# Entry of a hybrid encoder layer in another order: projections of the first half of the tokens ahead of the norm of the second, and a norm by square root and one Newton step

## The chip, the cores and the metric

The program runs on one core of one Trainium2 chip. The metric is the device time of one execution, in microseconds. The kernel before was timed three times: 1414.19, 1415.23 and 1418.97 us, median 1415.23 us.

## The reference

One layer of an encoder over 1024 tokens with 1024 channels, then a last norm. What matters here is the way in:

```
h = rms_norm(x, g_mix[l])
z = h @ w_in[l]
u_fn, q, k, v, u_ssm, gate_logits = jnp.split(z, splits, axis=-1)
y_fn = fourier_mix(u_fn) @ w_br_fn[l]
y_na = neighbourhood_attention(q * q_scale, k, v, na_rpb[l]) @ w_br_na[l]
y_ssm = ssm_branch(u_ssm, ssm_a_re[l], ...) @ w_br_ssm[l]
merged = gates[:, :, 0] * y_fn + gates[:, :, 1] * y_na + gates[:, :, 2] * y_ssm
x = x + merged @ w_out[l]
h = rms_norm(x, g_ffn[l])
x = x + jnp.square(jax.nn.relu(h @ w_up[l])) @ w_down[l]
```

rms_norm divides a token by the root of the mean of its squares. ssm_branch turns its parameters (log step, decay, B, C) into complex powers and phases, independent of x, and then scans the input u_ssm over the tokens.

## The kernel before

Each fp32 product is made of three matmuls in a rounded format: an operand is cut into a high part (a cast on ScalarE, ACT) and a low part (a subtraction on VectorE, DVE), `w_cut` for weights (L142, L143), `norm_b` for activations (L199, L200). Tokens lie in eight tiles of 128, in two halves of four.

The entry of `run` does this for each half: `norm_a` per tile (a Square with a row sum on ACT, L219; the inverse root on DVE, L208 to L212; a scaling in place on DVE, L221), `norm_b` per group of 128 channels (four transposes on TensorE, PE, L228, then the cut into hT), and the projection of the state space input u (two weights, 48 matmuls, `proj`), whose result ACT copies to uT (L940). Then come eight tiles of attention values v, 24 matmuls each, and then the gate logits and the rest.

The inverse root `rstd` is an integer estimate and three Newton steps on DVE, seven small instructions after the scale, eight in all.

The state space branch is a generator, `ssm`, that the main loop steps: 0.4 steps for every third matmul. Its first part, `ssm_params`, is some 110 operations on [128, 16] numbers, nearly all on GpSimd (POOL), each waiting for the one before; they begin when the parameters ssv have been loaded. Where DVE continues that chain, its first instruction is the complex square of L356 (recorded as L239), which uses the scratch columns T(4) and T(5) that POOL's last products (L239 to L244) use. The phases (`ssm_turn_a`, `ssm_turn_b`: tiles ef, en, E) go through DVE and ACT beside it.

All loads go through SyncE's queue (SP) in the order of issue. Weights are loaded into four buffers of their own (`wp`).

Every engine runs its own instructions in a fixed order. That order isn't the order of the source text: when the program is built, a planner with a timing model of its own orders each engine's instructions, and an engine that waits at one instruction holds up all behind it.

Of the kernel before, what the change touches and what calls it, by code (L numbers as in the profile page):

```python
# [23 lines left out]
NK = 128  # L24
# [40 lines left out]
class Trunk:  # L65
# [137 lines left out]
    def rstd(self, ss):  # L203


        V = self.nc.vector
        y, h, t = (self.tiny([P, 1], F32, x, 4) for x in ("ry", "rh", "rt"))
        V.tensor_scalar(out=h, in0=ss, scalar1=-0.5 / D, scalar2=-0.5 * EPS, op0=ALU.mult, op1=ALU.add)  # L208
        V.tensor_scalar(out=y.bitcast(I32), in0=h.bitcast(I32), scalar1=-0.5, scalar2=519526879.0, op0=ALU.mult, op1=ALU.add)
        for _ in range(3):  # L210
            V.scalar_tensor_tensor(out=t, in0=y, scalar=h, in1=y, op0=ALU.mult, op1=ALU.mult)
            V.scalar_tensor_tensor(out=y, in0=t, scalar=1.5, in1=y, op0=ALU.add, op1=ALU.mult)  # L212
        return y

    def norm_a(self, x, h=None):

        q = self.s([P, D], F32, "h") if h is None else h
        ss = self.tiny([P, 1], F32, "ss", 4)
        self.nc.scalar.activation(q, x, AF.Square, accum_out=ss)  # L219
        h = x if h is None else h  # L220
        self.nc.vector.tensor_scalar_mul(h, x, self.rstd(ss))  # L221
        return h
# [44 lines left out]
    def ssm_params(self):  # L267
# [46 lines left out]
        sn, sh, cs = T(6), T(7), T(8)  # L314
        nc.scalar.activation(sn, w, AF.Sin)
        nc.scalar.activation(sh, w, AF.Sin, scale=0.5)
        for q in range(4):
            self.ssm_turn_b(q)
        TT(T(4), sh, sh, ALU.mult)
        TS(cs, T(4), -2.0, 1.0, ALU.mult, ALU.add)  # L320
        lr, li = T(9), T(10)
# [98 lines left out]
    def ssm_prep(self, q):  # L420

        nc, V, G, A = self.nc, self.nc.vector, self.nc.gpsimd, self.nc.scalar
        g0 = 4 * q
        gs = slice(g0, g0 + 4)
        pa, bbar, bhat = self.ssm_pa, self.ssm_bb, self.ssm_bh

        def product(out, x, y, sh):

            t = self.m(sh, F32, "pt")
            V.tensor_tensor(out=t, in0=x[1], in1=y[1], op=ALU.mult)  # L430
            V.tensor_tensor(out=out[:, 0], in0=x[0], in1=y[0], op=ALU.mult)
            yield
            V.tensor_tensor(out=out[:, 0], in0=out[:, 0], in1=t, op=ALU.subtract)
            V.tensor_tensor(out=t, in0=x[1], in1=y[0], op=ALU.mult)
            yield
            V.tensor_tensor(out=out[:, 1], in0=x[0], in1=y[-1], op=ALU.mult)
            V.tensor_tensor(out=out[:, 1], in0=out[:, 1], in1=t, op=ALU.subtract if len(y) == 3 else ALU.add)
            yield

        U = self.m([P, 4, NK], F32, "U")  # L440
        self.dma(U, self.u_scr[64 * q:64 * q + 64].rearrange("(g c) (s k) -> (c s) g k", g=4, k=NK))
        AA = self.s([P, 2, 4, 8, 16], F32, "AA")
        sh = [P, 4, 8, 16]
        yield from product(AA, [self.ssm_cc[:, i, gs, :].unsqueeze(2).to_broadcast(sh) for i in range(2)],
                           [pa[:, i, gs, :].unsqueeze(3).to_broadcast(sh) for i in range(3)], sh)
        BB = self.s([P, 2, 4, 16, 8], F32, "BB")
        sh = [P, 4, 16, 8]
        yield from product(BB, [bhat[:, i, gs, :].unsqueeze(3).to_broadcast(sh) for i in range(2)],
                           [pa[:, i, gs, ::-1].unsqueeze(2).to_broadcast(sh) for i in range(2)], sh)
        AA = AA.rearrange("p i g s c -> p i g (s c)")  # L450
        bz = self.m([P, 2, 4, 64], F32, "bz")
        G.memset(bz, 0.0)
        for i in range(2):
            A.copy(bz[0:64, i, :, 0:16], bbar[0:64, i, gs, :])
            A.copy(bz[64:128, i, :, 32:48], bbar[64:128, i, gs, :])
        yield
        for _ in range(6 if q == 0 else 0):
            yield
        BT = self.s([P, 4, 2, P], F32, "BT")
        for b in range(2):  # L460
            ps = self.ps([P, 2, 2, P])
            for j in range(2):
                for i in range(2):
                    nc.tensor.transpose(ps[:, j, i, :], BB[:, i, 2 * b + j].rearrange("p c s -> p (c s)"), self.ident)  # L464
            A.copy(BT[:, 2 * b:2 * b + 2], ps)
# [12 lines left out]
        V.tensor_tensor(out=kp[:, :, 7, :], in0=kp[:, :, 7, :], in1=kt, op=ALU.add)  # L478
        yield
        M = self.m([P, 4, P], F32, "M")  # L480
        for s in range(8):
            self.dma(M[s::8], kp[:, :, 7 - s:15 - s, :].rearrange("p g t c -> p g (t c)"))
        yield
        self.ssm_mat[q] = (AA, BT, M, U)

    def ssm_data(self, q):
# [24 lines left out]
        V.tensor_tensor(out=ta, in0=ta, in1=tb, op=ALU.add)  # L511
        V.tensor_tensor(out=tc_, in0=tc_, in1=td, op=ALU.subtract)
        yield
        zs = [self.m(sh, F32, "z") for _ in range(2)]
        for v, z in ((ta, zs[0]), (tc_, zs[1])):
            V.tensor_tensor_scan(out=flat(z)[0:64, 1:L], data0=flat(rz)[0:64, 0:L - 1], data1=flat(v)[0:64, 0:L - 1],
                                 initial=0.0, op0=ALU.mult, op1=ALU.add)
# [3 lines left out]
                                 data1=flat(v)[64:128, 1:L][:, ::-1], initial=0.0, op0=ALU.mult, op1=ALU.add)  # L521
            V.memset(z[64:128, :, NK - 1], 0.0)
            yield
        V.tensor_tensor(out=ta, in0=zs[0], in1=E[:, 0], op=ALU.mult)
        V.tensor_tensor(out=tb, in0=zs[1], in1=E[:, 1], op=ALU.mult)
        yield
        V.tensor_tensor(out=td, in0=zs[1], in1=E[:, 0], op=ALU.mult)
        V.tensor_tensor(out=tc_, in0=zs[0], in1=E[:, 1], op=ALU.mult)
        yield
        V.tensor_tensor(out=ta, in0=ta, in1=tb, op=ALU.subtract)  # L530
        V.tensor_tensor(out=tc_, in0=tc_, in1=td, op=ALU.add)
# [35 lines left out]
    def ssm(self):  # L567
# [7 lines left out]
                yield from self.ssm_prep(q)  # L575

        def data():
            for q in range(4):
                while q not in self.ssm_mat:
                    yield  # L580
                yield from self.ssm_data(q)
# [314 lines left out]
    def run(self):  # L896
# [11 lines left out]
        def load_x():  # L908
            xs.append(self.s([P, D], F32, "x"))
            t = len(xs) - 1  # L910
            self.dma(xs[t], self.a["x"][t * P:(t + 1) * P, :])

        load_x()
        self.consts()
        for _ in range(3):
            load_x()
        self.w_raw(0)
        self.w_raw(1)
        for _ in range(4):
            load_x()  # L920
        hT = []
        uts = [self.s([P, 8, NK], F32, "uT") for _ in range(2)]
        for t in range(4):
            self.norm_a(xs[t])
        self.w_cut(0)
        for half in range(2):
            hT.append(self.act_tiles(half, "hT"))
            for k in range(8):
                self.norm_b(xs[4 * half:4 * half + 4], hT, half, k, self.gs[:, 0])
                if half == 0 and k == 3:  # L930
                    self.w_cut(1)
            xs[4 * half:4 * half + 4] = [None] * 4
            if half == 0:
                ws = self.w_next(2, 0, 1)
                for t in range(4, 8):
                    self.norm_a(xs[t])

            for i in range(2):
                ps = self.proj(ws[i], hT, half)
                A.copy(uts[i][:, :, 64 * half:64 * half + 64].rearrange("p s k -> p k s"), ps.rearrange("p (k s) -> p k s", s=8))  # L940
        ssm = Side(self.ssm(), 0.4)
        del xs
        for i in range(2):
            self.dma(self.u_scr[P * i:P * i + P], uts[i].rearrange("p s k -> p (s k)"))
        del uts, ws

        wv = self.w_next(4, 1, 2)
        self.sides.append(ssm)
        for t in range(8):
# [13 lines left out]
        del wv, rh, rl  # L963

        heads = {}

# [654 lines left out]
```

## Time and profile before

| | |
|---|---|
| median of the runs | 1415.23 us |
| profiled execution | 1414.49 us |
| its span in the trace | 1412.7 us |
| PE busy | 1378.5 us, 98% |
| DVE, ACT, POOL busy | 67%, 41%, 12% |

The span is the time from the first to the last instruction of the trace; 1.8 us of the profiled execution lie outside it. A time stamp below is in us from the start of the span. Instructions of one engine in the timeline may overlap by some hundredths, since they are pipelined.

### The profile page before, as it was taken

Reading aid. Unit: us, or ns where it says so; the run is one execution under the profiler, and the core shown is the slowest. Engines: PE = TensorE matmul, PEld = TensorE weight load, DVE = VectorE, ACT = ScalarE, POOL = GpSimd, SP = SyncE. Lnnn points to the kernel's source line nnn. Section 1 sums busy time; section 2 is a strip of 40 time slices with the busy share of each in tenths; the row PEclk is TensorE's granted clock in tenths of the full one; section 3 lists DMA queues with packets and bytes.
Section 4 is the critical chain, followed back from the end, with each engine's and each line's share of the span. In section 5 each row is a group of like instructions: output and inputs, shape, how many; then the busy total and the mean of one; then the engine's idle time right before and its main releaser. Section 6 shows DMA issues by size and latency. Waiting matters only on the chain.

```text
span 1412.7 us, 18521 instructions
## 1 busy us (share of the span) xinstructions
PE 1378.5 (98%) x6520; PEld 1150.1 (81%) x6520; DVE 952.8 (67%) x1812; ACT 577.0 (41%) x1103; POOL 166.8 (12%) x345
## 2 busy tenths in 40 slices
PE   6999999999999999999999999999999999999997
PEld 5788878888888888888788788888888788888885
DVE  6768788767562315443516897677777999878667
ACT  5523464766552212122403664233333454444244
POOL 3800122322200000000000012121121100000000
PEclk9999999999999999999999999999999999999999
DMA  6352546665652219111433125444448886363303
GB/s 230 107 161 83 171 120 196 187 176 154 210 194 98 100 45 331 57 56 49 136 111 142 68 90 202 148 164 144 154 149 282 282 278 199 118 191 127 97 9 119
DMA packets 103436, 209.65 MB, mean 148 GB/s; under 512 B 18224, under 2 KB 34992, under 8 KB 103344
## 3 DMA queue, kind: packets, MB, share of 16 engines
q1 hardware_dynamic: 79872, 153.10, 33.2%
q0 software_dynamic: 23472, 55.38, 12.0%
q8 instruction: 51, 0.84, 0.2%
q14 instruction: 41, 0.34, 0.1%
HBM read 146.52 MB, written 56.62 MB: 144 GB/s over the span
## 4 chain that ended last, share of the span: by engine, by line
PE 71%; issue 18%; POOL 5%; DVE 2%; DMA 2%; ACT 1%; SPq 0%; POOLq 0%; DVEq 0%
PE ps L171 42%; PE ps L165 25%; POOL h_scr L1300 4%; PE ps L792 1%; PE ps L809 1%; PE ps L813 1%; DMA ssv<-in_ssm_v 1%; DMA wr<-in_w_in 1%; SPq L111 0%; PE ps L1088 0%; DMA yT<-y_scr 0%; POOL pt L249 0%; DMA h_scr<-hs 0%; PE ps L464 0%; POOL pt L250 0%
## 5 line engine op out<-in xcount | busy, mean ns | idle before, releaser
L165 PE MATMUL ps<-dw,dh 128*128 128x512 f32 x1344 | 306.1, 390 | 2.3 <-DVE dw L197 2.3
L165 PE MATMUL ps<-fb,uw 128*128 128x512 f32 x1344 | 306.6, 390 | 1.4 <-DVE t L1147 1.0
L165 PEld LDWEIGHTS ps<-dw,dh 128*128 128x128 f32 x1344 | 252.1, 188 | 55.6 <-DVE dw L197 3.1
L165 PEld LDWEIGHTS ps<-fb,uw 128*128 128x128 f32 x1344 | 252.0, 188 | 54.5 <-PE ps L1088 1.2
L171 PE MATMUL ps<-hTh,wh 128*128 128x512 f32 x576 | 231.5, 403 | 3.2 <-DVE hTl L200 1.6
L171 PE MATMUL ps<-hTl,wh 128*128 128x512 f32 x576 | 227.1, 395 | 1.3 <-DVE hTl L200 1.3
L171 PE MATMUL ps<-hTh,wl 128*128 128x512 f32 x576 | 227.5, 395 | 0.0
L171 PEld LDWEIGHTS ps<-hTh,wh 128*128 128x128 f32 x576 | 109.3, 190 | 24.2 <-ACT wh L142 2.4
L171 PEld LDWEIGHTS ps<-hTh,wl 128*128 128x128 f32 x576 | 108.9, 189 | 23.0 <-issue 0.2
L171 PEld LDWEIGHTS ps<-hTl,wh 128*128 128x128 f32 x576 | 109.1, 189 | 20.9 <-DVE hTl L200 1.8
L143 DVE TENSOR_TENSOR wl<-wr,wh 128x1024 fp32r<-128x1024 f32 (+2 forms) x76 | 70.7, 942 | 60.2 <-ACT wh L142 57.4
L196 ACT CAST dh<-da 128x512 fp32r<-128x512 f32 x112 | 69.4, 620 | 96.9 <-PE ps L165 61.2
L1384 DVE TENSOR_TENSOR x<-x,ps 128x512 f32<-128x512 f32 x112 | 73.8, 687 | 33.8 <-PE ps L165 33.7
L197 DVE TENSOR_TENSOR dh<-da,dh 128x512 fp32r<-128x512 f32 x112 | 77.4, 691 | 14.9 <-ACT dh L196 14.8
L1300 POOL DMA_DIRECT2D h_scr<-hx x48 | 26.0, 541 | 495.6 <-ACT hx L1270 375.5
L171 PE MATMUL ps<-act,wh 128*128 128x512 f32 x256 | 78.7, 390 | 0.1
L142 ACT CAST wh<-wr 128x1024 fp32r<-128x1024 f32 (+2 forms) x76 | 60.7, 821 | 32.3 <-PE ps L171 8.3
L196 ACT CAST uw<-us 128x512 fp32r<-128x512 f32 x64 | 38.1, 626 | 84.2 <-DVE us L1227 84.2
L1022 ACT ACTIVATE tg<-ps 128x512 f32<-128x512 f32 x32 | 19.1, 597 | 123.9 <-PE ps L171 118.5
L1272 DVE SCALAR_TENSOR_TENSOR hx<-hx 128x512 f32<-128x512 f32 x52 | 35.8, 689 | 40.2 <-ACT hx L1264 39.7
L196 ACT CAST dw<-wd 128x512 fp32r<-128x512 f32 x80 | 49.4, 618 | 19.1 <-PE ps L165 18.4
L171 PEld LDWEIGHTS ps<-act,wh 128*128 128x128 f32 x256 | 47.7, 188 | 10.0 <-ACT wh L142 0.5
(288 smaller groups left out, 2092.5 us busy)
## 6 DMA issues: line engine op xcount, KB each, us to landing
da<-h_scr SPq DMA_DIRECT2D x112, 256.0 KB, 3.4
wr<-in_w_in SPq DMA_DIRECT2D x36, 512.0 KB, 4.4
wu<-in_w_up SPq DMA_DIRECT2D x32, 512.0 KB, 3.6
h_scr<-hs POOLq DMA_DIRECT2D x64, 256.0 KB, 2.6
wd<-in_w_down SPq DMA_DIRECT2D x64, 256.0 KB, 3.8
bm<-in_rpb POOLq DMA_DIRECT2D x64, 192.0 KB, 4.8
h_scr<-hx POOLq DMA_DIRECT2D x48, 256.0 KB, 2.7
vj<-v_scr POOLq DMA_DIRECT2D x32, 256.0 KB, 6.5
```

The lines of the kernel that those rows point to most:

```text
L142: self.nc.scalar.copy(hi, r)
L143: self.nc.vector.tensor_tensor(out=lo, in0=r, in1=hi.bitcast(F32), op=ALU.subtract)
L165: self.nc.tensor.matmul(out=out, lhsT=l, rhs=r, start=start and i == 0, stop=stop and i == last, skip_group_check=more)
L171: self.nc.tensor.matmul(out=out, lhsT=l, rhs=r, start=i == 0, stop=i == last)
L196: nc.scalar.copy(hi, src)
L197: nc.vector.tensor_tensor(out=lo, in0=src, in1=hi.bitcast(F32), op=ALU.subtract)
L792: nc.tensor.transpose(ps[:, i, :], sm[:, i * P:(i + 1) * P], self.ident)
L809: nc.tensor.matmul(out=ps, lhsT=v, rhs=two[i][x], start=i == 0 and x == 0, stop=False)
L1022: A.activation(tg, ps, AF.Tanh, scale=0.5)
L1272: V.scalar_tensor_tensor(out=x, in0=x, scalar=0.0, in1=x, op0=ALU.max, op1=ALU.mult)
L1300: self.nc.gpsimd.dma_start(out=self.t.h_scr[c, j - 1], in_=x)
L1384: self.nc.vector.tensor_tensor(out=self.x1[t][:, cs], in0=self.x1[t][:, cs], in1=self.banks[j][q], op=ALU.add)
```

## The change

The first four tiles of x are loaded, then two weights for u, then the parameters of the state space branch, then two weights for v; the other four tiles of x are loaded later. The order in the source is now: norm of the first half, u of the first half, v of the first tile, v of tiles 1 to 3 with the norm of the second half stepped in between as a side generator, u of the second half, v of tiles 4 to 7. The state space branch is stepped by hand in the entry, and its part that needs u waits for a flag. The inverse root is now a Sqrt on ACT, a reciprocal on DVE and one Newton step; a Sqrt of a constant stands at the start of the kernel, ahead of all data. Squares go to buffers that are there anyway. In the scan of the state space branch two buffers are saved.

```diff
--- before.py
+++ after.py
@@ -206,15 +206,15 @@
         V.tensor_scalar(out=h, in0=ss, scalar1=-0.5 / D, scalar2=-0.5 * EPS, op0=ALU.mult, op1=ALU.add)
-        V.tensor_scalar(out=y.bitcast(I32), in0=h.bitcast(I32), scalar1=-0.5, scalar2=519526879.0, op0=ALU.mult, op1=ALU.add)
-        for _ in range(3):
-            V.scalar_tensor_tensor(out=t, in0=y, scalar=h, in1=y, op0=ALU.mult, op1=ALU.mult)
-            V.scalar_tensor_tensor(out=y, in0=t, scalar=1.5, in1=y, op0=ALU.add, op1=ALU.mult)
+        self.nc.scalar.activation(y, h, AF.Sqrt, scale=-2.0)
+        V.reciprocal(y, y)
+        V.scalar_tensor_tensor(out=t, in0=y, scalar=h, in1=y, op0=ALU.mult, op1=ALU.mult)
+        V.scalar_tensor_tensor(out=y, in0=t, scalar=1.5, in1=y, op0=ALU.add, op1=ALU.mult)
         return y
...
@@ -454,8 +450,11 @@
-        for _ in range(6 if q == 0 else 0):
+        while not self.u_done:
             yield
+        U = self.m([P, 4, NK], F32, "U")
+        self.dma(U, self.u_scr[64 * q:64 * q + 64].rearrange("(g c) (s k) -> (c s) g k", g=4, k=NK))
...
@@ -910,43 +914,41 @@
+        one = self.tiny([P, 1], F32, "one", 1)
+        V.memset(one, 1.0)
+        A.activation(one, one, AF.Sqrt)
         load_x()
         self.consts()
         for _ in range(3):
             load_x()
         self.w_raw(0)
         self.w_raw(1)
-        for _ in range(4):
-            load_x()
-        hT = []
+        ssm = Side(self.ssm(), 0.4)
+        ssm.step()
+        self.w_raw(2)
+        self.w_raw(3)
+        self.u_done = False
+        hT = [self.act_tiles(0, "hT")]
         uts = [self.s([P, 8, NK], F32, "uT") for _ in range(2)]
         for t in range(4):
-            self.norm_a(xs[t])
+            self.norm_a(xs[t], q=uts[0].rearrange("p s k -> p (s k)"))
         self.w_cut(0)
...
+        def second():
+
+            for t in range(4, 8):
+                self.norm_a(xs[t], q=self.wp.tile([P, D], F32, tag="w", name=self.name("h")))
+                yield
+            for _ in range(4):
+                yield
+            for k in range(8):
+                self.norm_b(xs[4:8], hT, 1, k, self.gs[:, 0])
+                yield
+
+        u_in(0)
+        wv = self.w_next(4, 0, 0)
+        for t in range(4):
+            if t == 1:
+                for _ in range(4):
+                    load_x()
+                hT.append(self.act_tiles(1, "hT"))
+                norm2 = self.side(second(), 0.67)
+            if t > 0:
+                ssm.step()
+            v_in(t)
+        norm2.finish()
+        del xs
+        ssm.step()
+        ssm.step()
+        self.sides.append(ssm)
+        u_in(1)
+        for i in range(2):
+            self.dma(self.u_scr[P * i:P * i + P], uts[i].rearrange("p s k -> p (s k)"))
+        del uts, ws
+        self.u_done = True
+        for t in range(4, 8):
+            if t == 5:
+                self.w_ahead(1, 2)
+            v_in(t)
```

On DVE, this is where the scaling of the first tile of the second half and the state space chain stood before (x_89 is that tile; ry its inverse root; ef, en, E the phases; pt the parameters):

```order
L221 TENSOR_SCALAR x_89<-x_89,ry_236 128x1024
...
L221 TENSOR_SCALAR x_95<-x_95,ry_281 128x1024
L200 SCALAR_TENSOR_TENSOR hTl_346<-ps_353,gs_77,hTh_345 128x512
L402 TENSOR_TENSOR ef_588<-ssk_513,konst_75 128x512
...
L404 TENSOR_SCALAR en_607<-en_607 128x512
L239 TENSOR_TENSOR pt_511<-pt_511 128x16
```

And now (x_366 is the same tile, wl the low part of a weight for v, vt the values of the first tile, pa the powers at the chain's end):

```order
L400 TENSOR_TENSOR ef_428<-ssk_102,konst_78 128x512
L403 TENSOR_TENSOR ef_416<-ef_416,en_417 128x512
L143 TENSOR_TENSOR wl_322<-wr_143,wh_321 128x1024
...
L197 TENSOR_TENSOR vt_362<-ps_337,vt_362 128x8x64
L239 TENSOR_TENSOR pt_100<-pt_100 128x16
...
L366 TENSOR_SCALAR pa_704<-pa_704 128x128
L221 TENSOR_SCALAR x_366<-x_366,ry_444 128x1024
```

The scaling of the second half's tiles stood ahead of the first instruction of the phases and now stands behind the chain's DVE part, from L239 to L366; the first weight for v is cut behind the first phases.

On PE, the end of the first u before, and what follows it (ps_353 and its like are transposes of the second half):

```order
L171 MATMUL ps_319<-hTl_170,wh_199 128x512
L171 MATMUL ps_319<-hTh_169,wl_200 128x512
L228 MATMUL ps_353<-konst_75,x_89 128x128
L228 MATMUL ps_360<-konst_75,x_89 128x128
L228 MATMUL ps_367<-konst_75,x_89 128x128
```

And now the place where the second half's transposes begin, which is behind the first three tiles of v (ps_337, ps_434, ps_530; ps_603 is the fourth):

```order
L171 MATMUL ps_530<-wl_334,hTh_153 128x512
L171 MATMUL ps_530<-wh_333,hTl_154 128x512
L228 MATMUL ps_549<-konst_78,x_366 128x128
L228 MATMUL ps_559<-konst_78,x_366 128x128
L171 MATMUL ps_603<-wh_321,hTh_147 128x512
```

The 72 matmuls of three tiles of v now stand between the first u and the first transpose of the second half; the fourth tile's matmuls, the second u and the other four tiles stand behind it.

## Rows read from the trace of the kernel before

**Rows 1.** The page: busy us of each engine, share of the span, and number of instructions.

```profile
PE 1378.5 (98%) x6520; PEld 1150.1 (81%) x6520; DVE 952.8 (67%) x1812; ACT 577.0 (41%) x1103; POOL 166.8 (12%) x345
```

**Rows 2.** The waits of PE over the whole span: who, for whom, us in total, times, longest.

```profile
PE ps L228 <- DVE rh L208: 10.0, 1, 10.0
PE ps L171 <- DVE hTl L200: 2.9, 3, 1.3
PE ps L792 <- DVE mx L767: 1.1, 1, 1.1
PE ps L809 <- ACT sm L774: 0.8, 1, 0.8
PE ps L792 <- DVE sm L784: 0.6, 1, 0.6
```

**Rows 3.** Stretches of one us: their length, busy time of PE, PEld, DVE, ACT and POOL with counts, granted clock of PE (1.00 is 2.4 GHz, 0.50 is 1.2 GHz), DMA share, GB/s.

```profile
36.00:37.00 1.00, 0.00 (x0) 0.00 (x0) 1.00 (x3) 1.00 (x3) 0.83 (x3) 1.00 0.04 8
38.00:39.00 1.00, 1.00 (x4) 0.81 (x3) 1.00 (x4) 0.98 (x2) 0.83 (x3) 0.50 0.00 0
40.00:41.00 1.00, 1.00 (x4) 0.81 (x3) 1.00 (x4) 1.00 (x2) 0.75 (x4) 0.59 0.04 8
...
191.00:192.00 1.00, 0.61 (x3) 0.64 (x4) 0.97 (x3) 0.95 (x4) 0.87 (x2) 0.51 0.00 0
197.00:198.00 1.00, 1.00 (x4) 0.78 (x3) 1.00 (x1) 0.00 (x0) 0.00 (x0) 0.58 0.00 0
```

**Rows 4.** The timeline of PE: start, busy time, instruction, count, and in brackets the idle time before it and what ended it. The last row is the first matmul behind all values.

```profile
18.75 0.50 PE L171 MATMUL ps<-hTh,wh 128*128 128x512 f32 x1 [0.80 <-DVE hTl L200]
...
29.77 3.98 PE L228 MATMUL ps<-konst,x 128*128 128x128 f32 x32
34.55 0.50 PE L171 MATMUL ps<-hTh,wh 128*128 128x512 f32 x1 [0.80 <-DVE hTl L200]
...
87.25 1.96 PE L165 MATMUL ps<-AA,bz 128*64 128x128 f32 x16
...
95.41 0.39 PE L171 MATMUL ps<-hTh,wh 128*128 128x512 f32 x1
```

**Rows 5.** The timeline of DVE in the first norm: the second Newton step of the first tile, the next tile's first instruction, the low part of the first weight, and the scaling of the fourth tile.

```profile
6.37 0.22 DVE L211 SCALAR_TENSOR_TENSOR rt<-ry,rh 128x1 f32<-128x1 f32 x1
8.48 0.15 DVE L208 TENSOR_SCALAR rh<-ss 128x1 f32<-128x1 f32 x1 [1.89 <-ACT h L219]
...
12.59 1.22 DVE L143 TENSOR_TENSOR wl<-wr,wh 128x1024 fp32r<-128x1024 f32 x1
...
15.17 0.75 DVE L221 TENSOR_SCALAR x<-x,ry 128x1024 f32<-128x1024 f32 x1
```

**Rows 6.** SP's issues of loads (start and length of the issue), and the chain that ended last (start, length): the load of the first weight and that of the parameters, each from issue to landing.

```profile
4.62 3.00 SPq L111 DMA_DIRECT2D x<-in_x  x4
...
11.09 0.33 SPq L111 DMA_DIRECT2D ssv<-in_ssm_v  x1
...
3.54 7.53 DMA wr<-in_w_in
11.09 9.20 DMA ssv<-in_ssm_v
```

**Rows 7.** The timeline of POOL in the parameter chain: its first instruction, two that follow each other beside a DVE instruction that reads PSUM, one beside a DVE weight cut, and its last before the products on larger tiles.

```profile
20.38 0.20 POOL L256 TENSOR_SCALAR pt<-ssv 128x16 f32<-128x16 f32 x1 [18.43 <-DMA ssv<-in_ssm_v]
...
41.53 0.22 POOL L250 TENSOR_TENSOR pt<-pt 128x16 f32<-128x16 f32 x1
41.84 0.30 POOL L249 TENSOR_SCALAR pt<-pt 128x16 f32<-128x16 f32 x1
...
44.63 1.02 POOL L250 TENSOR_TENSOR pt<-pt 128x16 f32<-128x16 f32 x1
...
62.44 0.22 POOL L244 TENSOR_TENSOR pt<-pt 128x16 f32<-128x16 f32 x1
```

**Rows 8.** The timeline of DVE where it goes on with that chain, and a stretch in which it works beside POOL.

```profile
43.22 2.35 DVE L143 TENSOR_TENSOR wl<-wr,wh 128x1024 fp32r<-128x1024 f32 x2
...
62.69 0.58 DVE L239 TENSOR_TENSOR pt<-pt 128x16 f32<-128x16 f32 x1 [6.26 <-POOL pt L244]
63.28 1.11 DVE L405 TENSOR_TENSOR ef<-ef,en 128x512 f32<-128x512 f32 x1
...
68.28 0.68 DVE L197 TENSOR_TENSOR vt<-ps,vt 128x512 fp32r<-128x512 f32 x1
69.15 0.42 DVE L417 TENSOR_SCALAR E<-en 128x512 f32<-128x512 f32 x1
71.48 0.23 DVE L368 TENSOR_SCALAR pa<-pa 128x128 f32<-128x128 f32 x1
```

**Rows 9.** The timeline of ACT: copies of u, a cast of a weight for v, a load of a function table, and the wait of a Sin for POOL.

```profile
29.51 2.00 ACT L940 COPY uT<-ps 128x512 f32<-128x512 f32 x2 [2.46 <-PE ps L171]
...
37.60 1.09 ACT L142 CAST wh<-wr 128x1024 fp32r<-128x1024 f32 x1
38.70 1.28 ACT L316 ACT_TABLE_LOAD   x1
40.00 0.22 ACT L316 ACTIVATE pt<-pt 128x16 f32<-128x16 f32 x1
...
46.62 0.22 ACT L315 ACTIVATE pt<-pt 128x16 f32<-128x16 f32 x1 [3.58 <-POOL pt L249]
```

More of the change, by code (lines that the diff above doesn't have):

```diff
@@ L208, in rstd, with norm_a @@
         V.tensor_scalar(out=h, in0=ss, scalar1=-0.5 / D, scalar2=-0.5 * EPS, op0=ALU.mult, op1=ALU.add)
-        V.tensor_scalar(out=y.bitcast(I32), in0=h.bitcast(I32), scalar1=-0.5, scalar2=519526879.0, op0=ALU.mult, op1=ALU.add)
-        for _ in range(3):
-            V.scalar_tensor_tensor(out=t, in0=y, scalar=h, in1=y, op0=ALU.mult, op1=ALU.mult)
-            V.scalar_tensor_tensor(out=y, in0=t, scalar=1.5, in1=y, op0=ALU.add, op1=ALU.mult)
-        return y
-    def norm_a(self, x, h=None):
-        q = self.s([P, D], F32, "h") if h is None else h
+        self.nc.scalar.activation(y, h, AF.Sqrt, scale=-2.0)
+        V.reciprocal(y, y)
+        V.scalar_tensor_tensor(out=t, in0=y, scalar=h, in1=y, op0=ALU.mult, op1=ALU.mult)
+        V.scalar_tensor_tensor(out=y, in0=t, scalar=1.5, in1=y, op0=ALU.add, op1=ALU.mult)
+        return y
+    def norm_a(self, x, h=None, q=None):
+        q = h if q is None else q
         ss = self.tiny([P, 1], F32, "ss", 4)
@@ L316, in ssm_params @@
         nc.scalar.activation(sh, w, AF.Sin, scale=0.5)
-        for q in range(4):
-            self.ssm_turn_b(q)
         TT(T(4), sh, sh, ALU.mult)
@@ L438, in product @@
             yield
-        U = self.m([P, 4, NK], F32, "U")
-        self.dma(U, self.u_scr[64 * q:64 * q + 64].rearrange("(g c) (s k) -> (c s) g k", g=4, k=NK))
         AA = self.s([P, 2, 4, 8, 16], F32, "AA")
@@ L513, in ssm_data @@
         yield
-        zs = [self.m(sh, F32, "z") for _ in range(2)]
+        zs = [tb, td]
         for v, z in ((ta, zs[0]), (tc_, zs[1])):
@@ L523, in ssm_data @@
             yield
-        V.tensor_tensor(out=ta, in0=zs[0], in1=E[:, 0], op=ALU.mult)
-        V.tensor_tensor(out=tb, in0=zs[1], in1=E[:, 1], op=ALU.mult)
+        V.tensor_tensor(out=ta, in0=tb, in1=E[:, 0], op=ALU.mult)
+        V.tensor_tensor(out=tc_, in0=tb, in1=E[:, 1], op=ALU.mult)
         yield
-        V.tensor_tensor(out=td, in0=zs[1], in1=E[:, 0], op=ALU.mult)
-        V.tensor_tensor(out=tc_, in0=zs[0], in1=E[:, 1], op=ALU.mult)
+        V.tensor_tensor(out=tb, in0=td, in1=E[:, 1], op=ALU.mult)
+        V.tensor_tensor(out=td, in0=td, in1=E[:, 0], op=ALU.mult)
         yield
@@ L577, in data @@
         def data():
+            while not self.u_done:
+                yield
+            for q in range(4):
+                self.ssm_turn_b(q)
+                yield
             for q in range(4):
@@ L918, in run, with u_in @@
         self.w_raw(1)
-        for _ in range(4):
-            load_x()
-        hT = []
+        ssm = Side(self.ssm(), 0.4)
[4 more added lines that the diff above has]
+        hT = [self.act_tiles(0, "hT")]
         uts = [self.s([P, 8, NK], F32, "uT") for _ in range(2)]
         for t in range(4):
-            self.norm_a(xs[t])
+            self.norm_a(xs[t], q=uts[0].rearrange("p s k -> p (s k)"))
         self.w_cut(0)
[L926 to L936, printed above, removed]
+        for k in range(8):
+            self.norm_b(xs[0:4], hT, 0, k, self.gs[:, 0])
+            if k == 3:
+                self.w_cut(1)
+        xs[0:4] = [None] * 4
+        ws = self.w_next(2, 0, 4)
+        def u_in(half):
             for i in range(2):
@@ L940, in run, with v_in @@
                 A.copy(uts[i][:, :, 64 * half:64 * half + 64].rearrange("p s k -> p k s"), ps.rearrange("p (k s) -> p k s", s=8))
[L941 to L949, printed above, removed]
+        def v_in(t):
             half, c0 = t // 4, (t % 4) * P
@@ L962, in run @@
                      vt.rearrange("p h i c -> p h (i c)").bitcast(F32))
-        del wv, rh, rl
+        def second():
+            for t in range(4, 8):
+                self.norm_a(xs[t], q=self.wp.tile([P, D], F32, tag="w", name=self.name("h")))
+                yield
+            for _ in range(4):
+                yield
+            for k in range(8):
+                self.norm_b(xs[4:8], hT, 1, k, self.gs[:, 0])
+                yield
+        u_in(0)
[23 more added lines that the diff above has]
+            v_in(t)
+        del wv
         heads = {}
```

## Prediction

> **What bounds the kernel now.** The page comes first: PE is busy for 1378.5 of 1412.7 us, the other engines have room [rows 1]. So a change can win only what PE idles or runs at half clock, and loses whatever it makes PE idle anew. The view of PE's waits says where it idles: 10.0 us until the first transpose, 2.9 us for low parts of hT in the entry, and 2.5 us in one place of the attention [rows 2]. The stretches of one us add the clock: after the wait at 36 us the granted clock is 0.50 until 41 us, after the attention's waits it is 0.51 at 191 and 0.58 at 197 us [rows 3]. A stretch of 3.5 us at half clock costs some 1.7 us, the attention's near 7 us some 3.2 us. Last come the timelines: the first u runs at 18.75 to 29.77 us, 48 matmuls, 0.23 us each; then 32 transposes in 3.98 us, the second u from 34.55 us, and the values end at 95.41 us [rows 4]. The same timelines show that POOL's chain of parameters, not PE, sets when DVE and ACT go on: DVE waits 6.26 us for POOL [rows 8], a Sin 3.58 us [rows 9]. In the kernel before nothing that PE needs soon stands behind the DVE wait: the second half was scaled long before.
>
> **The norm itself.** Three Newton steps become one, with a Sqrt and a reciprocal: eight DVE instructions become four, and ACT gets one. Before, DVE stops in the middle of the first tile's steps, since the next tile's instruction stands there and waits 1.89 us for data [rows 5]; that goes, but the fourth tile counts. Its Square ends at some 11 us either way. Now the low part of the first weight (1.22 us, behind its cast) stands ahead of its scaling, so the scaling starts at about 14 us instead of 15.17 [rows 5]. The first matmul then comes at 17.5 instead of 18.75 us: 1.2 us won (bounds: nothing, if that cut is as late as before; 3 us, if it was the only delay), and u ends at 28.5 us. Sixteen norms lose some 60 tiny DVE instructions; the eight of the second norm lie behind matmuls either way, and I take nothing for them.
>
> **Loads.** The parameters ssv are issued where the first of the late x tiles was, at 4.62 instead of 11.09 us. Ahead of them is the second weight, behind the first, which lands at 11.07 us [rows 6]; 512 KB more is 1.25 us at the 420 GB/s that the load of x0 to w1 shows as one estimate from those bytes and that time, so ssv lands at about 12.6 instead of 20.3 us. The late x tiles are issued behind the fourth weight for v, which needs the buffer of the second, free at some 20 us; they land before 30 us, except the last, which stands behind the store of the first values on SP and lands near 53 us. None of that is late, by what follows. The two weights for v that come before them are in time as well.
>
> **The parameter chain.** POOL's part begins at 20.38 and ends at 62.66 us: 42.3 us [rows 7]. Beginning at 12.6 it ends at 54.9 us. Bounds: some 110 instructions, undisturbed one per 0.31 us (41.53 to 41.84), would take 34 us and end at 46.7; beside a DVE weight cut one takes 1.02 us [rows 7, 8], and DVE now has the phases and four weight cuts in one block just where the second exponential runs, so up to 3 us more, 57.9 us. I take the same length as before, since as many such DVE instructions stand beside it.
>
> **DVE behind it.** The order of DVE now has the chain's DVE part, from L239 to L366, ahead of x_366, the first tile of the second half. Before, that part ran from 62.69 to 71.71 us, 9.0 us [rows 8]. Out of it come a phase instruction (1.1), two of E (0.4 each) and one cut of values (0.7), in come nine tiny ones of the norms at 0.1: some 7.3 us. With the scaling (0.75) x_366 is ready at 54.9 + 7.3 + 0.7 = 62.9 us. Behind the waiting L239 stand that scaling, all four tiles, and the low parts of the second hT.
>
> **PE meanwhile.** After u (28.5 us) it needs the first weight for v. On ACT the cast stands behind both copies of u: 2.0 + 1.1 us [rows 9], 31.6 us; on DVE its low part stands behind the first phases, which wait for POOL's second exponential, 34 to 35 us. Then 72 matmuls take 16.6 us, and 1.7 us for half clock: PE is through with three tiles of v at 50 to 53 us. The next instruction in its order is the transpose of x_366. PE waits there for some 10 us, with 24 matmuls of the fourth tile behind the waiting transpose. This also swallows the 1.2 us from the start.
>
> **The sum.** At 62.9 us the kernel before had 95.4 - 62.9 = 32.5 us to the end of the values. The changed one has 24 + 48 + 96 = 168 matmuls, 38.6 us, the transposes, 4.0 us, the same 2.0 us of state space matmuls [rows 4], 1.7 us for half clock after the wait, and some 1.0 us in which the last two transposes wait for PSUM banks (eight are in use; before 0.80 and up to 1.3 us were lost there [rows 2, 4]): 47.3 us. That is 14.8 us behind. With POOL at its lower bound, L239 waits for the first values instead (48 us), x_366 comes at 56.0, and the loss is 7.9 us; at the upper one it is 17.8 us.
>
> **Later.** From 95 us on PE hardly waits before, so a delay stays, unless waits later go. In the attention 2.5 us of waits and 3.2 us of half clock can go at most, 5.7 us; as the order there is new and the same DVE instructions compete, it may as well become 2 us worse. The order after the change again has a stretch there without projections between the small matmuls. I take 2 us won. The table loads: two more in the entry and one at the second norm, 1.28 us each [rows 9], while ACT waits anyway. The sum goes against the profiled execution, 1414.49 us, 0.7 us below the median of the runs: 1414.5 + 14.8 - 2 = 1427 us.
>
> **A rule on the port.** The row: beside a DVE cut POOL's instruction takes 1.02 us, beside one that reads PSUM 0.22 us [rows 7, 8]. The Trainium skill, GPSIMD Engine Reference, Specifications, says that GpSimd shares its SBUF interfaces with VectorE and is held up by DVE instructions with two SBUF inputs or in a two-port mode. By that rule all the phases and cuts hold POOL up, one behind another, and the chain would stand at its upper bound; that is the second rival.
>
> **Rivals.** (1) POOL isn't what PE waits for. If its last L244 came by 42 us and ACT had the squares done early, x_366 would be scaled by 50 us, PE would go on from 50 with 45 us of work, and the entry would end where it ended, at 95; with the attention's 5.7 us gone as well, 1409 us: faster. For it speaks that the chain starts 8 us earlier; against it that even undisturbed it ends at 46.7. (2) The port decides: 17.8 behind, 1430 us. (3) The chain runs near its lower bound, and ACT becomes the gate: values copied at 48, two squares, a table load of 1.28 us, a Sqrt, then the scaling: x_366 at 53 to 56 us, 5 to 8 us behind, 1417 to 1421 us with the later gain or without. For it speaks that DVE idles between its cuts; against it that the DVE part after POOL alone takes 7 us. The Trainium skill, ScalarE: Activation LUTs, What ACT_TABLE_LOAD costs, counts about 2.66 us for each switch of function set, drain included, and by that this rival's time would be 1.4 us longer; the trace shows 1.30 us from the load's start to the next activation [rows 9].
>
> **Chances.** The forecast 0.65 (1421 to 1433 us), rival 1 0.07, rival 2 0.14, rival 3 0.14. About 0.3%, 4.2 us, is what a measurement of this kernel can tell from no change, so the bounds are 1411 and 1419.5. Faster: most of rival 1, 0.06. Same: the rest of it, two thirds of rival 3 and the best of the forecast's own spread, 0.14. Slower: 0.80. The range 1415 to 1433 holds rival 3's lower end with later gains and rival 2 with a worse attention. The forecast's own range is 1421 to 1433.
>
> **What would show it.** In the profile after, the waits of PE must have one of 8 us or more at L228 for DVE's scaling (L221) near 53 to 63 us, DVE an idle of several us at its first L239 for POOL's L244, and the granted clock must be 0.50 behind both. POOL's first instruction must stand near 12.6 us, the first matmul near 17.5, the values must end near 110. It is wrong if PE has no wait of over 3 us between 45 and 65 us, or if POOL's last L244 lies before 47 us. If the values end at 110 and the time still is not slower, the later waits have paid for it, and their rows must be gone.

## The result, and the profile after

The changed kernel takes 1433.41 us (median; 1432.33 to 1433.65), the kernel before, timed beside it, 1415.88 us: ratio 1.0127, 95% interval 1.0115 to 1.0139. The forecast was 1427 us with a range to 1433: the direction is right, the time lies 0.4 us outside the range. The profiled execution after took 1432.33 us, its span 1430.5 us, 17.8 us more than before.

First the page, busy time of each engine, which answers to [rows 1]: PE is 3.2 us busier, so the other 14.6 us are idle time.

```profile
PE 1381.7 (97%) x6520; PEld 1150.5 (80%) x6520; DVE 945.7 (66%) x1749; ACT 582.2 (41%) x1123; POOL 165.7 (12%) x345
```

The waits of PE over the span, which answer to [rows 2] (who, for whom, us in total, times, longest): the first wait is new, the second is mostly the wait until the first transpose (7.3 us, 10.0 before), the third grew from 1.6 us, and the last three stand in the attention.

```profile
PE ps L228 <- DVE ry L212: 10.2, 1, 10.2
PE ps L228 <- DVE x L221: 7.7, 2, 7.3
PE ps L171 <- ACT wh L142: 6.6, 3, 5.0
...
PE ps L813 <- ACT p L196: 1.3, 1, 1.3
PE ps L796 <- ACT sm L786: 1.1, 1, 1.1
...
PE ps L796 <- DVE v L507: 1.0, 1, 1.0
```

The first of these three stood there before too. Its line of the kernel before isn't among those of [rows 2], so that PE's waits in the attention were 4.3 us in all and not 2.5:

```profile
PE ps L809 <- ACT p L196: 1.6, 1, 1.6
```

The timeline of PE, which answers to [rows 4]: the first matmul of u and of v, the first transpose of the second half, a block of state space matmuls that before stood behind all values, the first matmul behind all values, the first Fourier product.

```profile
16.89 0.50 PE L171 MATMUL ps<-hTh,wh 128*128 128x512 f32 x1 [0.74 <-DVE hTl L200]
33.10 1.65 PE L171 MATMUL ps<-wh,hTh 128*128 128x512 f32 x3 [5.00 <-ACT wh L142]
63.09 0.66 PE L228 MATMUL ps<-konst,x 128*128 128x128 f32 x2 [10.15 <-DVE ry L212]
...
104.36 1.05 PE L165 MATMUL ps<-U,BT 128*128 128x128 f32 x8
112.98 0.39 PE L171 MATMUL ps<-hTh,wh 128*128 128x512 f32 x1
...
432.98 0.40 PE L165 MATMUL ps<-ct,fh 128*128 128x256 f32 x2
```

The last of these in the kernel before:

```profile
415.54 0.40 PE L165 MATMUL ps<-ct,fh 128*128 128x256 f32 x2
```

The values end 17.57 us later (95.41 before). But two blocks of eight U,BT matmuls, 0.8 us each (104.36 to 105.17), now stand ahead of this mark, so the entry proper lost 16.0 us. The first Fourier product comes 17.44 us later; between the marks there are 1.6 us less of work, so that stretch lost 1.5 us. The rest of the span adds 0.4 us.

Stretches of time of PE, which answer to [rows 3] (length, PE busy, granted clock, DMA share, GB/s): idle and half clock go together in both new waits.

```profile
33.00:34.00 1.00, 0.90 (x2) 0.50 0.00 0
57.00:58.00 1.00, 0.00 (x0) 0.50 0.00 0
...
0.00:120.00 120.00, 93.66 (x425) 0.93 0.41 136
120.00:450.00 330.00, 323.49 (x1773) 0.99 0.58 167
```

Up to 120 us PE idles 26.3 us, against 14.2 before; summing busy time times missing clock over such rows of one us gives 4.6 us of half clock, against 1.7. Between 120 and 450 us PE idles 6.5 us, against 4.3, and half clock costs 1.7 us, against 2.9.

The timelines of POOL, DVE and ACT, which answer to [rows 7 to 9]: the chain's first and last instruction, what waits for its end on DVE, the scaling of x_366, and two waits of ACT.

```profile
12.89 1.30 POOL L256 TENSOR_SCALAR pt<-ssv 128x16 f32<-128x16 f32 x1 [10.94 <-DMA ssv<-in_ssm_v]
54.17 0.22 POOL L244 TENSOR_TENSOR pt<-pt 128x16 f32<-128x16 f32 x1
...
54.43 0.57 DVE L239 TENSOR_TENSOR pt<-pt 128x16 f32<-128x16 f32 x1 [5.13 <-POOL pt L244]
62.06 0.22 DVE L366 TENSOR_SCALAR pa<-pa 128x128 f32<-128x128 f32 x1
62.19 0.75 DVE L221 TENSOR_SCALAR x<-x,ry 128x1024 f32<-128x1024 f32 x1
...
30.14 0.22 ACT L316 ACTIVATE pt<-pt 128x16 f32<-128x16 f32 x1 [7.80 <-DVE zi L264]
59.69 0.20 ACT L209 ACTIVATE ry<-rh 128x1 f32<-128x1 f32 x1 [5.24 <-DVE rh L208]
```

x_366 is ready at 62.94 us (62.9 was forecast). The Sin at 30.14 us was not foreseen: it waits 7.80 us for a step of POOL's second exponential, whose scratch column T(7) it overwrites, and the copies of u and the first weight's cast stand behind it.

### The profile page after: what moved, and what is told of

Its sections match the earlier page's. It is cut to its first block, busy times and chain, and to the rows that moved or that the text cites. A ratio compares the mean times of both kernels' runs of the same rounds, so it can differ in the third digit from the quotient of the medians.

```text
span 1430.5 us, 18470 instructions
## 1 busy us (share of the span) xinstructions
PE 1381.7 (97%) x6520; PEld 1150.5 (80%) x6520; DVE 945.7 (66%) x1749; ACT 582.2 (41%) x1123; POOL 165.7 (12%) x345
## 4 chain that ended last, share of the span: by engine, by line
PE 68%; issue 19%; POOL 6%; DVE 3%; DMA 2%; ACT 2%; SPq 0%; POOLq 0%; ACTq 0%; DVEq 0%
PE ps L171 40%; PE ps L165 24%; POOL h_scr L1339 4%; PE ps L796 1%; PE ps L813 1%; DMA x<-in_x 1%; PE ps L817 1%; DMA b_scr<-spl 0%; PE ps L228 0%; POOL pt L250 0%; POOL pt L249 0%; PE ps L1127 0%; PE ps L463 0%; ACT wh L142 0%; ACT uT L219 0%
## 5 line engine op out<-in xcount | busy, mean ns | idle before, releaser
L165 PEld LDWEIGHTS ps<-fb,uw 128*128 128x128 f32 x1344 | 251.9, 188 | 54.4 <-PE ps L1127 1.2
L171 PEld LDWEIGHTS ps<-hTh,wl 128*128 128x128 f32 x576 | 108.6, 189 | 22.9
```

Source lines behind the costliest of these rows:

```text
L165: self.nc.tensor.matmul(out=out, lhsT=l, rhs=r, start=start and i == 0, stop=stop and i == last, skip_group_check=more)
L171: self.nc.tensor.matmul(out=out, lhsT=l, rhs=r, start=i == 0, stop=i == last)
```

## The experiments

The theory at the start (order theory): the loss is made where x_366's scaling stands on DVE behind POOL's chain. Ratios below are to the kernel before, timed beside each group.

**The new root alone.** The kernel before, with the change's L209 to L212 in place of its own root, and the square root of a constant at the start.

```diff
+        self.nc.scalar.activation(y, h, AF.Sqrt, scale=-2.0)
+        V.reciprocal(y, y)
...
```

> The kernel before with the new inverse root alone (square root, reciprocal, one Newton step; the square root of a constant at the start). Order theory (the loss is made by the place of the second half's scaling on DVE, behind the chain of parameters): the root alone costs little, 1411 to 1418 us, 1414 at best guess, with the first matmul some 1 us earlier. Root theory (table loads and hops between DVE and ACT make the loss): 1422 us or more.

Measured: 1415.25 us, ratio 1.0002 (0.9993 to 1.0012). The root theory falls. The first matmul did not come earlier, though (18.79 us against 18.75):

```profile
18.79 0.50 PE L171 MATMUL ps<-hTh,wh 128*128 128x512 f32 x1 [0.79 <-DVE hTl L200]
```

**The change with the old root.**

```diff
-        self.nc.scalar.activation(y, h, AF.Sqrt, scale=-2.0)
-        V.reciprocal(y, y)
+        V.tensor_scalar(out=y.bitcast(I32), in0=h.bitcast(I32), scalar1=-0.5, scalar2=519526879.0, op0=ALU.mult, op1=ALU.add)
+        for _ in range(3):
...
```

> The changed kernel with the old inverse root (integer estimate, three Newton steps). Its DVE order still has the chain's DVE part ahead of the second half's scaling, so the order theory expects the wait of PE for x_366 again, 8 us or more, and 1429 to 1438 us. Root theory: most of the loss goes, 1416 to 1422 us.

Measured: 1437.25 us, ratio 1.0149 (1.0134 to 1.0164). In the new order the new root is worth some 3 us (1.0149 against 1.0127): with the old one the first matmul comes 3.0 us later, and PE takes up x_366 at 68.5 us instead of 63.1.

```profile
19.89 0.50 PE L171 MATMUL ps<-hTh,wh 128*128 128x512 f32 x1 [0.80 <-DVE hTl L200]
...
68.48 0.66 PE L228 MATMUL ps<-konst,x 128*128 128x128 f32 x2 [12.61 <-DVE ry L212]
```

**The late x tiles loaded early:** first ahead of the parameters, as in the diff, then, in a second run, behind `self.w_raw(3)`.

```diff
+        for _ in range(4):
+            load_x()
         ssm = Side(self.ssm(), 0.4)
...
-                for _ in range(4):
-                    load_x()
```

> The changed kernel with the four late tiles of x loaded ahead of the parameters, as before the change. In its DVE order the scaling of the second half now stands ahead of the chain's DVE part. Order theory: no wait of PE over 3 us between 45 and 65 us, the 10 us and some 1.7 us of half clock go, other waits grow by 1 to 4 us: 1419 to 1427 us, 1423 at best guess. Attention theory (most of the loss is made later): 1429 us or more. Load theory (x is simply there too late) also expects a fast run here; the next kernel parts the two.

> The changed kernel with the four late tiles of x loaded right behind the fourth weight instead of behind the first values' store; its DVE order still has the chain's DVE part (L239) ahead of the second half's scaling. Order theory: the wait of PE for that scaling stays at 7 us or more, 1428 to 1436 us. Load theory: x is there early, so the wait goes, 1419 to 1425 us.

Measured: 1426.29 us, ratio 1.0073 (1.0058 to 1.0088), and 1435.53 us, 1.0138 (1.0120 to 1.0157). In both, x is in memory early; only where the planner also put its scaling ahead of the chain is there a gain. In the second, x is loaded from 12 us on and scaled at 64.66 us, behind L239 at 59.41 us. But the wait at the transposes is 3.2 us there, not 7: PE came late itself. Its first transpose stands at 16.82 us instead of 7.30, since the planner put the first weight's cast ahead of three of the first half's squares on ACT, and the cast of the first weight for v held it up 9.80 us. So this run does not show the wait that was expected of it, and its time falls into the expected range for other reasons as well; it does show that x is scaled late though it was loaded early. PE's timeline of the second:

```profile
46.33 1.65 PE L171 MATMUL ps<-wh,hTh 128*128 128x512 f32 x3 [9.80 <-ACT wh L142]
65.54 0.30 PE L228 MATMUL ps<-konst,x 128*128 128x128 f32 x1 [2.00 <-DVE rt L211]
66.99 0.41 PE L228 MATMUL ps<-konst,x 128*128 128x128 f32 x1 [1.15 <-DVE x L221]
```

In the first, 11 us of loss remain. Its waits of PE up to 120 us have no single large one behind the start:

```profile
PE ps L228 <- DVE x L221: 4.3, 2, 3.1
PE ps L171 <- ACT wh L142: 2.4, 1, 2.4
PE ps L171 <- DVE wl L143: 2.0, 1, 2.0
```

Its ACT timeline shows why x is still late there (3.1 us): first a Sin of the chain waits 4.07 us for POOL, then the Sqrt of the second half alternates with the Sin of the phases, three loads of a table in 6 us.

```profile
45.34 0.22 ACT L315 ACTIVATE pt<-pt 128x16 f32<-128x16 f32 x1 [4.07 <-POOL pt L249]
...
46.10 1.28 ACT L209 ACT_TABLE_LOAD   x1
47.39 0.20 ACT L209 ACTIVATE ry<-rh 128x1 f32<-128x1 f32 x1
...
48.32 1.28 ACT L413 ACT_TABLE_LOAD   x1
...
50.26 1.28 ACT L209 ACT_TABLE_LOAD   x1
```

**Parameters loaded later as well.** x early, and the parameters behind the fourth weight:

```diff
+        for _ in range(4):
+            load_x()
+        self.w_raw(2)
+        self.w_raw(3)
         ssm = Side(self.ssm(), 0.4)
         ssm.step()
-        self.w_raw(2)
-        self.w_raw(3)
...
```

> The changed kernel with the late x tiles loaded early and the parameters loaded behind the fourth weight, so the chain on POOL starts about where it did before the change. The DVE order has the second half's scaling ahead of the chain's DVE part, and on ACT the casts of the weights for v stand right behind the copies of u, ahead of the Sin. Order theory: no wait over 4 us on PE between the first matmul and the end of the values, 1413 to 1420 us, 1417 at best guess. Theory that the sequence of the entry itself (values before the second norm) costs: 1424 us or more.

Measured: 1429.04 us, ratio 1.0094 (1.0079 to 1.0109): a miss for the order theory in its simple form; the other one, that the sequence itself costs, had 1424 us or more. x is scaled in time, but now the low parts of the second hT stand behind the chain's continuation, and PE waits for those, as the timelines of PE and DVE show:

```profile
67.42 0.66 PE L228 MATMUL ps<-konst,x 128*128 128x128 f32 x4 [3.25 <-DVE hTl L200]
...
63.97 0.57 DVE L239 TENSOR_TENSOR pt<-pt 128x16 f32<-128x16 f32 x1 [6.56 <-POOL pt L244]
66.62 0.74 DVE L200 SCALAR_TENSOR_TENSOR hTl<-ps,gs,hTh 128x512 fp32r<-128x512 f32 x1
```

**A longer chain.**

```diff
         TT(qi, qi, den, ALU.mult)
+        for _ in range(12):
+            TS(cs, cs, 1.0, None, ALU.mult, None)
```

> The changed kernel with twelve more instructions on [128, 16] numbers in POOL's chain (multiplications by one, behind the products with den), at 0.31 to 0.37 us each 3.7 to 4.4 us. Order theory: POOL's last product of the chain ends 3.7 to 4.4 us later, the wait of PE at x_366 grows from 10.2 to 13 to 14.6 us (a few DVE instructions fewer stand between the two, up to 0.9 us back), the wait of 5 us for the weight's cast stays, and the time is 1436 to 1438 us. If the chain is not what is waited for: 1433 us, no change.

Measured: 1432.13 us, ratio 1.0118 (1.0101 to 1.0135): no change against the changed kernel, so the expectation failed. POOL's chain did end 3.1 us later, but the planner, which saw the longer chain too, put the scaling 5.1 us behind L239 instead of 7.8. x_366 came 0.4 us later. An edit that changes the planner's inputs does not test a fixed order; the next ones force it.

```profile
57.55 0.57 DVE L239 TENSOR_TENSOR pt<-pt 128x16 f32<-128x16 f32 x1 [5.25 <-POOL pt L244]
62.64 0.74 DVE L221 TENSOR_SCALAR x<-x,ry 128x1024 f32<-128x1024 f32 x1
```

**The scan's buffers.** The change with its old buffers, and the kernel before with the new ones:

```diff
-        zs = [self.m(sh, F32, "z") for _ in range(2)]
+        zs = [tb, td]
...
```

> The changed kernel with the scan's two buffers as before. Order theory: the entry is untouched; the 1.5 us that the stretch from the end of the values to the first Fourier product became longer belong to the new order of the attention's start, 1431 to 1435 us. Buffer theory: the saved buffers make the late waits in the attention, 1428 to 1431 us.

> The kernel before with the scan's saved buffers alone. Both theories of the entry: 1413 to 1417 us, no change. Buffer theory: 2 us or more slower, 1417 to 1420 us, with new waits behind 180 us.

Measured: 1432.73 us, ratio 1.0123 (1.0108 to 1.0138), and 1414.53 us, 0.9993 (0.9983 to 1.0004). In neither kernel do the buffers make a difference that a measurement tells, so the expected 2 us or more are not theirs.

**The scaling forced ahead of the chain.** Tiny instructions that read the scaled tiles and write the chain's scratch columns, so that the planner can't put the chain's continuation first; in the first run one column, T(4), in the second both. `self.x2` holds the four tiles.

```diff
+        for xt in self.x2:
+            for o in (T(4), T(5)):
+                V.tensor_scalar(out=o, in0=xt[:, 0:16], scalar1=0.0, scalar2=None, op0=ALU.mult)
         self.cmul(l2, (lr, li), (lr, li), T(4), T(5), V, V)
...
```

> The changed kernel with four tiny DVE instructions that read the four scaled tiles of the second half and write the chain's scratch column, so on DVE the second half's scaling must stand ahead of the chain's continuation (L239); the orders of ACT and DVE ahead of that are as in the changed kernel. The run with the longer chain left the time as it was, so the place on DVE and not the chain's end is to be shown. Order theory: x_366 is ready at 55 to 57 us (squares 53.2, table load, Sqrt, 1 us of DVE), PE waits there 2 to 4 us instead of 10, less half clock: 1423 to 1428 us. Rival (x_366 comes late by itself, from load, squares and Sqrt): the wait stays over 7 us and the time over 1430 us.

> As the run with the scaling moved ahead, but both scratch columns of the chain are written by the tiny instructions, so that no instruction of the chain's continuation can stand ahead of x_366 and hold it up until POOL's last product (in that run one did, at 54.1 us). Order theory: x_366 is ready at 55.5 to 56.5 us, the wait of PE there is 2.5 to 3.5 us, and the time 1425 to 1428 us, 1 to 2.5 us below that run; some 10 us of loss are then left that the chain does not make (weights for v cast late, squares late, half clock). Rival (nothing is left to win there): the same time as that run.

Measured: 1428.54 us, ratio 1.0096 (1.0078 to 1.0114), and 1427.13 us, 1.0087 (1.0074 to 1.0100). The first lies 0.5 us above its range. The chain ahead of x_366 is worth some 6 us of the 17.5, give or take 2.5 us by the intervals. In the first run an instruction of the chain (L240, at 54.11 us) still stood ahead. In the second x_366 no longer waits for POOL, only for its squares, a table load, the Sqrt and DVE's own steps; it is ready at 57.08 us, and PE waits 3.92 us for it, both some 0.5 us more than expected. Its DVE and PE timelines:

```profile
55.07 0.16 DVE L210 RECIPROCAL ry<-ry 128x1 f32<-128x1 f32 x1 [1.36 <-ACT ry L209]
56.34 0.74 DVE L221 TENSOR_SCALAR x<-x,ry 128x1024 f32<-128x1024 f32 x1
...
57.22 0.66 PE L228 MATMUL ps<-konst,x 128*128 128x128 f32 x2 [3.92 <-DVE x L221]
...
33.14 1.65 PE L171 MATMUL ps<-wh,hTh 128*128 128x512 f32 x3 [5.00 <-ACT wh L142]
```

**The Sin forced behind the first cast,** alone and with the first form of the edit above. `o` is sn or sh, `wt` the first weight for v.

```diff
+        nc.scalar.copy(o, wt[0][:, 0, 0:16].bitcast(F32))
         nc.scalar.activation(sn, w, AF.Sin)
...
```

> The changed kernel with small copies that make the Sin of the parameter chain stand behind the cast of the first weight for v on ACT, so the copies of u and this cast no longer wait for POOL. The second half's scaling stays behind the chain. Order theory: the wait for the cast falls from 5.0 to 2.5 to 3.5 us, the wait at x_366 grows by as much, and the time stays: 1430 to 1435 us. If the wait for the cast is a loss of its own: 1428 to 1430 us.

> Both of these edits. Order theory: PE is through with three tiles of v some 2 us earlier, and x_366 is ready some 1 to 2 us earlier than with the scaling moved alone, as the squares follow the values: 1421 to 1427 us, below the run with the scaling moved alone by 1 to 2.5 us. If the two waits are one loss: the same time as that run.

Measured: 1430.73 us, ratio 1.0112 (1.0096 to 1.0128), and 1427.98 us, 1.0095 (1.0079 to 1.0111). The wait for the cast falls from 5.00 to 2.48 us, but another of 2.88 us for the low part (0.39 before the edit) follows at once: on DVE it stands behind the phases, which begin at 28.09 us, when POOL has their input, and last until 34.20 us. The time of the run with the Sin alone lies in its range, but the wait at x_366 fell to 7.11 us instead of growing: the planner put the scaling 5.8 us behind L239 (60.40 and 54.62 us) instead of 7.8. With both edits the time is that of the scaling moved alone: the 1 to 2.5 us more that were expected did not come. PE's timeline of the run with the Sin alone:

```profile
31.08 1.51 PE L171 MATMUL ps<-wh,hTh 128*128 128x512 f32 x3 [2.48 <-ACT wh L142]
35.47 0.79 PE L171 MATMUL ps<-wl,hTh 128*128 128x512 f32 x1 [2.88 <-DVE wl L143]
61.30 0.66 PE L228 MATMUL ps<-konst,x 128*128 128x128 f32 x2 [7.11 <-DVE rh L208]
```

**The state space edits alone,** in the kernel before, without empty steps of its generator, then with four, as in the diff, and with six. The late places of its second part of the phases and of its loads of u are those of the change.

```diff
-        for q in range(4):
-            self.ssm_turn_b(q)
...
+        for _ in range(4 if q == 0 else 0):
+            yield
         U = self.m([P, 4, NK], F32, "U")
         self.dma(U, self.u_scr[64 * q:64 * q + 64].rearrange("(g c) (s k) -> (c s) g k", g=4, k=NK))
```

> The kernel before with the change's edits of the state space branch alone: its phases' second part and its loads of u behind the parameters, the saved scan buffers; the entry stays. Order theory (the later loss comes with the entry's delay and the new order that follows from it): 1412 to 1417 us, idle time of PE behind 120 us as before, some 4.3 us. Rival (these edits make the attention's waits): idle time behind 120 us of 6 us or more and 1417 to 1420 us.

> The kernel before with the edits of the state space branch alone, and four empty steps ahead of its first load of u, so that on PE the first transposes of BB stand 24 matmuls later than without them (5.4 us; the wait for BB there was 5.4 us). If that wait and the waits of the attention are apart: the wait of 5.4 us falls to 0 to 1 us, the attention keeps an idle time of 1 to 2 us behind 120 us, 1408 to 1411 us, faster than the kernel before. If the attention's waits only come back when the start is not late: 1413 to 1416 us.

> The same with six empty steps, as the kernel before has for its first group; the first transposes of BB stand 39 matmuls (8.9 us) later. Same two theories: no wait for BB, 1408 to 1411 us, if the attention keeps its gain; 1413 to 1416 us if its waits come back.

Measured: 1416.86 us, ratio 1.0012 (1.0003 to 1.0021); 1414.60 us, 0.9995 (0.9986 to 1.0004); 1417.50 us, 1.0012 (1.0003 to 1.0021). The first run's time lies in the range of the order theory, but its waits fit neither expectation. Behind 120 us its PE idles only 1.35 us (4.3 before), but ahead of it there is a new wait of 5.4 us for BB. Its waits and windows:

```profile
PE ps L463 <- DVE BB L431: 5.4, 1, 5.4
...
120.00:450.00 330.00, 328.65 (x1821) 1.00 0.58 168
```

With four empty steps the wait for BB falls to 0.8 us and the idle time behind 120 us is 3.4 us again, as the second theory had it; with six it is 7.0 us, though that profile (1414.54 us) is the fastest of its runs, and the median lies above both ranges. So the waits of the attention aren't a property of an edit. They move by some 6 us with whatever shifts the order ahead of them, and what was won on one side came back on the other in these three runs. No version here beats the kernel before by more than a measurement tells.

## Why the prediction was wrong in size

**What held.** The mechanism of the sum, term by term: POOL's chain ran from 12.89 to 54.4 us (12.6 to 54.9 forecast), DVE's part behind it 7.8 us (54.43 to 62.28; 7.3 forecast), x_366 was ready at 62.94 us (62.9), PE was through with three tiles of v at 52.9 us (50 to 53) and waited 10.15 us (10). That x_366 came out to the tenth is luck: the chain began 0.3 us later, took 0.8 us less, and DVE's part took 0.5 us more. The weight's cast was the exception: 33.0 us instead of 31.6, because of the Sin ahead of the copies of u. That stayed without effect on the sum, as PE waited at x_366 anyway.

**The step that failed: "Later", "I take 2 us won".** Instead 1.5 us were lost up to the first Fourier product and 0.4 us behind: 3.8 us off, most of the 5.0 us by which the forecast change (12.8) falls short of the measured one (17.8, from profile to profile, of which 16.0 in the entry). The step took the place of old waits as room to win, and misread them: 2.5 us in one place, where the trace has 4.3 us in two (190 to 195 and 338 to 342 us). What it hoped for in half clock came in part (2.9 to 1.7 us), but the idle time grew by 2.2 us. The runs show that this stretch idles anything from 1.35 to 7.3 us (the latter with the scan's old buffers) with small shifts of the order; a term of that kind has no sign and belongs into the range alone.

**The second term that was mis-sized: "47.3 us" behind x_366.** It measured 63.09 to 112.98 less the 1.6 us of U,BT work, 48.3 us. The sum left out the eight transposes of BB (L463) in that stretch, some 0.8 us by an estimate (with six matmuls of 0.23 us they fill 91.11 to 93.30 us). With the 0.2 us until PE took x_366 up this makes 16.0 instead of 14.8 us.

**The rivals.** Rival 2 (1430 us) lies nearest in time and is wrong all the same: the chain took 41.5 us against 42.3 before, so it was not stretched, as the forecast had it. Nor had it reason to be: DVE had less to do beside it, 22.9 us against 30.2, with six weight cuts each time, as the two stretches show, before and after (length, then busy time of PE, PEld, DVE, ACT and POOL):

```profile
20.38:62.66 42.28, 40.04 (x185) 32.77 (x184) 30.20 (x80) 27.11 (x42) 35.50 (x113) 0.96 0.34 115
12.89:54.39 41.50, 33.84 (x136) 26.65 (x136) 22.92 (x42) 21.91 (x33) 34.72 (x113) 0.92 0.32 113
```

Single instructions were held up: the first took 1.30 us beside a weight cut on DVE (12.91 to 14.13 us), 0.20 before [rows 7]. The Trainium skill, GPSIMD Engine Reference, Specifications, names this contention of GpSimd with VectorE instructions that have two SBUF inputs; the single instruction agrees, and the length of the chain does not test it, as the cuts beside it were as many.

Rival 3 needed a chain near 34 us. Its picture, x_366 gated by ACT, came only where the scaling was forced ahead, at 57.1 us, and the time was 1427.1 us and not 1417 to 1421, because x_366 is not all that PE waits for.

Rival 1 and the argument under it, that without POOL's gate the entry would end where it ended, fell by experiment: with x_366 forced ahead of the chain the time is still 1427.1 us. About a third of the loss is the chain ahead of x_366. For the rest no run gives a single cause. Up to 120 us, that run still has 5.5 us more of idle time than the kernel before and 3.0 us more of half clock. With values ahead of the second norm, PE meets the weights for v right behind u (5.4 us of waits in that run, and nothing there before), then x_366 (3.9 us, its squares stand behind the casts of the values on ACT), each with its stretch of half clock. Of the 5.4 us about half comes by the Sin from POOL's chain again: in the four runs without the Sin ahead of the cast, PE waits 2.4 to 2.5 us for it, but in three of them 2.0 to 3.8 us more for the low part behind the phases. In the kernel before, the first weight for v was cast at 37.60 us [rows 9] and first used at 43.82 us; that the second half's norm and projection gave POOL, ACT and DVE the time for it is a reading of the two orders, and no run tests it alone. The 1.2 us from the new root, the forecast's one gain, came as 1.9 us (first matmul 16.89 us) and were swallowed, as forecast. That they are the root's in this order, and nothing in the old one, the two runs with the roots exchanged show.

**The table loads.** "While ACT waits anyway" held in the changed kernel, where ACT waits for DVE. In the run with x loaded early three of them stood between the Sins and the Sqrts, and x came late by them and by the Sin ahead. There the next activation starts 1.29 us after the load does (46.10 to 47.39), and the one ahead ended at 46.08 us. The Trainium skill, ScalarE: Activation LUTs, What ACT_TABLE_LOAD costs, gives about 2.66 us a switch with its drain; the trace does not agree, and the measurement decides.

**What stays open:** which instruction of the attention's order makes its waits come and go, and how the remaining 10 to 12 us divide between the late weights, the late squares and what follows; no run took away only one of those.

## What to carry to other kernels

When a gate on one engine is found, ask what stands next behind it before its removal is priced: here x_366, the weight's cast, its low part and the low parts of hT each took over as soon as the one ahead was moved, because the same chain on POOL holds ACT and DVE as well. Where a planner orders the instructions, an edit that should test an order has to force it by a data dependence, since the planner answers every other edit with a new order. And waits far behind the change are no reserve: put them into the range, with both signs.

## What the runs showed of the hardware that was not expected

DVE is held up by POOL as well as POOL by DVE. The chain's first products on DVE, 128x16, ran in the changed kernel beside POOL's products on [128, 256]:

```profile
55.73 0.70 DVE L243 TENSOR_TENSOR pt<-pt 128x16 f32<-128x16 f32 x1
...
55.65 0.75 POOL L241 TENSOR_TENSOR bbar<-tb 128x256 f32<-128x256 f32 x1
```

and in the run with the scaling forced ahead of them by both columns when POOL was through (its last ended at 59.9 us):

```profile
63.86 0.17 DVE L243 TENSOR_TENSOR pt<-pt 128x16 f32<-128x16 f32 x1
```

0.70 us against 0.17 us for the same instruction. Of the twelve such products five took 0.48 to 0.70 us in the one, and each of these five ended 0.03 us after a product of POOL's did (here 56.43 and 56.40 us); in the other all took 0.17 or 0.18 us.
